# Queries and keys projected transposed and loaded whole, and readers moved away from producers, in a hybrid decoder step

## The chip, the core and the metric

The kernel runs on one core of one Trainium2 chip. The metric is the time of one execution on the device in microseconds (us). Engines are named as the profile names them: PE is TensorE (PEld its weight loads), DVE is VectorE, ACT is ScalarE, POOL is GpSimd, SP is SyncE, which here only issues DMAs. Each engine executes its own queue in order.

## What is computed

One layer of a decoder for two groups of rows that share weights: a prompt of 1024 rows, and a sample of 8 rows, each with 8192 cached positions.

```python
q, k, v, logf, u, z = mixer_inputs(rmsnorm(xp, g_mix[l]), w_in[l], b_f[l], g_sgu_v[l])
xp = xp + merge_heads(fox_prompt(q, k, v, logf), sgu_prompt(u, z, w_s[l], b_s[l]),
                      g_att_out[l], g_sgu_out[l], w_o[l])
mk, mv = memory_kv(mem_prompt, g_mem[l], w_ck[l], w_cv[l])
xp = xp + cross_attend(rmsnorm(xp, g_cross[l]), mk, mv, w_cq[l], w_co[l])
f, conv_p = conv_ffn(rmsnorm(xp, g_ffn[l]), ...)      # width-3 convolution, silu(gate) * val
xp = xp + f
...
att = fox_sample(q, k, v, logf, cache_k[l], cache_v[l], cache_logf[l], page_table)   # the sample's rows
```

`fox_attend` adds the difference of two cumulative sums of `logf` to each score, masks causally and takes a softmax over 8 heads of 64. `sgu_prompt` mixes the rows of each 128-row chunk with a causal 128x128 matrix per head and multiplies by u. Cross attention has 4 heads of 256 over 256 memory rows. The width is 1024, the MLP's is 2816. Outputs are the rows, and also the prompt's keys, values, gates, memory keys and values, and the last convolution rows.

## The kernel before

**Arithmetic.** Everything is float32. A large product is made of three fp32r products: `split` writes a high part (ScalarE, L212 or, with a gain, L215) and a low part, the rest (VectorE, L213 or L216), and `gemm3` (L242 to L244) adds high x high, high x low and low x high. `wload` (L230) loads a weight tile and splits it. Smaller products and all transposes run in float32.

**Stages of the prompt.** `p1` projects the normalised input in five column ranges: q, then gates and u, then k, v and z. The input comes transposed (`load_x`, L318); the row factors come from a second, row-wise load (`stats`, L328, squared in L207). q, k, v and the gating values go to DRAM (`evac`, L384 and L385). The decode's 8 sample rows ride along as narrow products (`sample_mm`, L254); `sample_sum` copies their parts out of PSUM (L266) and adds them up with one more product (L268).

Then the prompt goes in two halves of 512 rows. `attention` takes pairs of heads: `load` fetches q, k and v of a pair by rows, `setup` transposes q and k on TensorE (L649, L672), copies high parts (L655, L656, L676, L680, and POOL's L678) and subtracts low parts (L657, L681), so that one product over 128 rows and one over 68 rows (L696, L698; the last four rows carry the gate sums, fetched in L658 and L667) give a score; the exponentials are L706, the turning of the weights L724, the product with v L740. The first half's attention is mixed with the memory projection `pmem` and with `gating(0)`. Per half there follow `merge` and `out_proj` (with w_o), `cross`, which ends in another `out_proj` (w_co), and `ffn`. `residual` (L880, L207) adds each output tile to the rows and squares it; `norm_T` scales the rows (L920, before the MLP alone), transposes them (L929, L936) and splits them with the gain (L215, L216). In `cross`, `weigh` makes one head's weights (keys transposed in L977, scores L991, exponentials L997, scaling L1000) and `gather` turns them (L1008), copies them (L1009) and multiplies by the values (L1014).

**The sample.** `decode` walks 8 x 16 pieces of the cache: `kstep` gathers keys (L1175), multiplies by the query (L1183, on VectorE, and for some of the first 50 pieces on POOL) and sums (L1187); `vstep` gathers values (L1236) for column-tiled products (L1242). `sample_rest` then runs the eight rows through the remaining layers, to L1537 and the store in L1545.

**Order.** Both are generators. The prompt's yields a number after each piece of work; the loop at the end adds these up, and whenever the sum passes `PACE` of the stage (6 to 20; 4.0 once `sample_rest` has begun) it issues one step of the sample's. `mix` interleaves a second prompt generator in the same way. What is issued is a priority: a planner with a model of the engines fixes each engine's order. `hold`, set in `out_proj` where `i >= HI`, would stop the background; `HI` is 9 and i at most 3.

**Buffers.** 18 tiles of 128x1024 (`U`), 7 of 128x520 (`T2`), 4 raw weight tiles (`WRAW`), 4 and 2 PSUM banks that `BK` hands out in turn, one (`MS`) and one (`DV`) for the sample.

Of the kernel before, what the change touches and what calls it, by code (L numbers as in the profile page):

```python
# [22 lines left out]
NB = 8  # L23
# [35 lines left out]
KP = 2  # L59
PW = 1  # L60
LD = [(0, 1, 0), (0, 0, 0)]
ST = [(0, 1, 1), (0, 1, 1)]
# [7 lines left out]
HI = 9  # L70
HK = 0
# [3 lines left out]
SB = 2  # L75
# [8 lines left out]
def build(nc, tc, ctx, a, phases=None):  # L84
# [97 lines left out]
    q_d = dram.tile([T, AW], F32, tag="q_d", name="q_d")  # L182
    k_d, v_d = a["o_k"], a["o_v"]
# [3 lines left out]
    cq_d = dram.tile([NH, 4, T], F32, tag="cq_d", name="cq_d")  # L187
    ck_d = dram.tile([NH, 4, T], F32, tag="ck_d", name="ck_d")
# [74 lines left out]
    def sample_sum(ps, n, tmp=T2):  # L263

        t = tmp(n)
        nc.scalar.activation(t, ps[:, :n], AF.Copy)  # L266
        ps2 = BK()
        mmul(ps2[:8, :n], selS, t, start=True, stop=True)  # L268
        return ps2[:8, :n]
# [27 lines left out]
    def newest(e):  # L297

        return next(i for i in reversed(nc.cur_bb.bb.instructions) if i.engine == e)


    def p1(early):
        rstd = const.tile([P, 8], F32, tag="rstd", name="rstd")
        rstd8 = const.tile([P, 8], F32, tag="rstd8", name="rstd8")
        ssx = sm([P, 8], "ssx", 1)
# [6 lines left out]
        xh, xl = [[U([P, T], F32R) for _ in range(8)] for _ in range(2)]  # L312

        def load_x(kk, hf):
# [8 lines left out]
        def stats(hf):  # L323
            for q in range(2):
                xr = KV().rearrange("p (c d) -> p c d", d=D)
                t0 = hf * 4 + q * 2
                with tc.issue_after(x_in):
                    nc.sync.dma_start(xr, a["x"][t0 * P : (t0 + 2) * P, :].rearrange("(c p) d -> p c d", p=P))  # L328
                for i in range(2):
                    ssq_into(ssx[:, t0 + i : t0 + i + 1], xr[:, i, :])  # L330
            c = slice(hf * 4, hf * 4 + 4)
            r = rstd_of(ssx[:, c], D, 4, "r4")
            nc.vector.tensor_copy(rstd[:, c], r)
            nc.vector.tensor_scalar(rstd8[:, c], r, 0.125, None, op0=ALU.mult)
# [11 lines left out]
        def loaded(c0, n, parts, first=False):  # L346
# [3 lines left out]
            for kk in range(4):  # L350
                if first:
                    load_x(kk, 0)
# [3 lines left out]
                ws.append(w_)  # L356
                if first and kk == 1:
# [3 lines left out]

        ws, sps = loaded(O_Q, 512, [(0, 512)], first=True)
        for kk in range(4):
            load_x(kk, 1)
        x_in = newest(ENG.SP)
# [9 lines left out]
        stats(0)  # L375
        stats(1)
        sp = sample_sum(*sps[0])
        qs = T2()[:8]
        nc.vector.tensor_scalar(qs, sp, rs8, None, op0=ALU.mult)
        nc.sync.dma_start(qs_d, qs)  # L380

        def evac(ps, dst, sc, tt):
            t = T2()
            nc.scalar.activation(t, ps, AF.Copy, scale=sc[:, tt : tt + 1])  # L384
            nc.scalar.dma_start(dst[tt * P : (tt + 1) * P, :], t)  # L385

# [13 lines left out]
        pss = yield from by_rows(0, ws)  # L400
        for tt in range(8):
            ps = BK() if tt > 3 else pss[tt]
            if tt > 3:
                mm_chunk(tt, ws, ps, 0, 512)
                yield 5.2
            evac(ps, q_d, rstd8, tt)
# [32 lines left out]
        def gate_rows():  # L439
# [3 lines left out]
            for hf in range(2):  # L443
# [11 lines left out]
                for r_, src in ((0, ch), (1, cl)):  # L455
                    nc.sync.dma_start(cq_d[:, r_, s], src.bitcast(F32))
                    nc.sync.dma_start(cq_d[:, 2 + r_, s], one)
                    nc.sync.dma_start(ck_d[:, r_, s], one)
                    ng = T2()[:8]
                    nc.vector.tensor_scalar(ng, src.bitcast(F32), -1.0, None, op0=ALU.mult)  # L460
                    nc.sync.dma_start(ck_d[:, 2 + r_, s], ng)


        for c0, dst in ((O_K, k_d), (O_V, v_d)):
            ws, sps = loaded(c0, 512, [(0, 512)])
            for tt in range(8):
                ps = BK()
                mm_chunk(tt, ws, ps, 0, 512)
# [14 lines left out]
                evac(ps, dst, rstd, tt)  # L483
# [9 lines left out]
        for tt in range(8):  # L493
            if tt < 4:
                ps = BK()
                mm_chunk(tt, ws, ps, 0, 512)
                if tt == SD:
# [37 lines left out]
    def gating(hf):  # L535
# [6 lines left out]
        for pr_ in range(2):  # L542
            z = U([P, 2, 512])
            u = U([P, 2, 512])
# [3 lines left out]
            nc.sync.dma_start(u, sgu_d[rows, :].rearrange("(c p) d -> p c d", p=P))  # L548
            for i in range(2):
# [3 lines left out]
            yield 1  # L553
# [36 lines left out]
    def pmem():  # L590
        rm = const.tile([P, 2], F32, tag="rm", name="rm")
        ssm = sm([P, 2], "ssm", 1)
        for mt in range(2):
            t = U([P, D])
            nc.sync.dma_start(t, a["mem"][mt * P : (mt + 1) * P, :])
            ssq_into(ssm[:, mt : mt + 1], t)
        r = rstd_of(ssm, D, 2, "r2")
        nc.vector.tensor_copy(rm, r)
        mh, ml = [], []
        for q in range(2):  # L600
            h, l = U([P, 4, 256], F32R), U([P, 4, 256], F32R)
            raw = WRAW(1024).rearrange("p (k m) -> p k m", m=256)
            nc.sync.dma_start(raw, a["memT"][q * 512 : (q + 1) * 512, :].rearrange("(k p) m -> p k m", p=P))
            for k in range(4):
                kk = q * 4 + k
                split(raw[:, k, :], h[:, k, :], l[:, k, :], scale=gp[:, G_MEM + kk : G_MEM + kk + 1])
            mh.append(h)
            ml.append(l)
        yield 0.1
# [19 lines left out]
    def attention(hf, late=None, at=3):  # L629
# [3 lines left out]
        def load(hp):  # L633
            cs = slice(hp * P, (hp + 1) * P)
            qn = T2().rearrange("p (i c) -> p i c", c=P)
            nc.sync.dma_start(qn, q_d[hf * 512 : (hf + 1) * 512, cs].rearrange("(i p) c -> p i c", p=P))
            if hf == 0:
                kvn = U([P, 2 * nk, P])
# [1099 lines left out]
```

## Time and profile before

| | |
|---|---|
| median of 3 runs | 1971.17 us (1969.85 to 1985.79) |
| the profiled execution | 1971.44 us, span 1969.6 us |
| granted PE clock, mean | 0.965 |
| PE, DVE, ACT, POOL busy | 93%, 71%, 37%, 27% |
| DMA | 517 MB, mean 263 GB/s |

Stages in the span, by the first and last instructions of their lines: `p1` 0 to 277 us, the attention of the first half to about 385 and of the second to about 546, cross attention's products with the memory 661 to 723 and 1360 to 1420, the first MLP 816 to 1242, the second 1483 to 1945. The sample's decode ends at about 1515 and its rest at 1965. A busy share counts an instruction that runs at the half clock as busy, so 93% of PE holds slow work too; the column PEclk of a stretch tells how much.

### The profile page before, as it was taken

What the parts mean: (1) busy time and instruction counts of PE and PEld (TensorE: products, weight loads), DVE (VectorE), ACT (ScalarE), POOL (GpSimd) and SP (SyncE); (2) the same over time, 40 slices, a digit from 0 to 9 for tenths busy, and PEclk for the clock granted to TensorE, in tenths of its full rate; (3) what the DMA queues carried; (4) which work ended last, traced back from release to release, by engine and by line L of the source; (5) the groups of instructions that cost most, each with busy time, mean ns of one, the idle gap of its engine ahead of it and who ended that gap; (6) DMA issues with size and microseconds to landing.
All of it is one profiled execution on the core that took longest, in us unless ns stands there. A gap on an engine that the chain in (4) does not pass through costs nothing.

```text
span 1969.6 us, 23939 instructions
## 1 busy us (share of the span) xinstructions
PE 1828.8 (93%) x9159; PEld 1295.1 (66%) x9159; DVE 1395.3 (71%) x1651; ACT 730.1 (37%) x1344; POOL 538.0 (27%) x376
## 2 busy tenths in 40 slices
PE   8899989878899789699999999998999999999997
PEld 5777766556666547477777776666567677667773
DVE  4877466786767798898989999988335549653442
ACT  5332246566723232332432332433324333242331
POOL 1664342342245433323234243333110000000000
PEclk9999989989999989899999999999999999999998
DMA  8766777654487898788778798989664458665755
GB/s 327 257 242 211 290 303 244 244 166 142 161 342 275 325 335 324 249 324 299 291 268 336 271 356 339 374 314 363 232 217 151 150 188 273 233 220 211 271 192 193
DMA packets 160466, 517.05 MB, mean 263 GB/s; under 512 B 20168, under 2 KB 41928, under 8 KB 127584
## 3 DMA queue, kind: packets, MB, share of 16 engines
q0 software_dynamic: 38528, 270.88, 36.5%
q1 hardware_dynamic: 114912, 232.06, 33.8%
q10 hardware_dynamic: 6912, 12.59, 1.7%
q8 instruction: 72, 1.18, 0.2%
q14 instruction: 42, 0.34, 0.0%
HBM read 493.63 MB, written 21.84 MB: 262 GB/s over the span
## 4 chain that ended last, share of the span: by engine, by line
PE 71%; DVE 10%; DMA 9%; issue 5%; ACT 3%; POOL 1%; SPq 0%; ACTq 0%; DVEq 0%; POOLq 0%
PE ba L242 12%; PE ba L243 12%; PE ba L244 12%; PE bb L242 6%; PE bb L243 5%; PE bb L244 5%; PE dv L1242 5%; DVE s L1187 2%; DMA wr<-w_in 2%; DVE kv L1183 2%; DMA kv<-cache_k,kidx 2%; DVE wl L213 1%; PE dv L1485 1%; DMA u<-zg_d 1%; PE ba L1014 1%
## 5 line engine op out<-in xcount | busy, mean ns | idle before, releaser
L212 ACT ACTIVATE wh<-wr 128x1024 fp32r<-128x1024 f32 (+2 forms) x220 | 228.9, 1044 | 506.7 <-PE ba L243 176.5
L213 DVE TENSOR_TENSOR wl<-wr,wh 128x1024 fp32r<-128x1024 f32 (+2 forms) x220 | 268.5, 1231 | 176.7 <-PE ba L244 70.1
L1187 DVE TENSOR_REDUCE s<-kv 128x32 f32<-128x2048 f32 (+1 forms) x139 | 292.1, 2107 | 18.0 <-POOL kv L1183 17.4
L1175 POOL DMA_INDIRECT kv<-cache_k,kidx x128 | 174.3, 1362 | 449.1 <-PE dv L1242 208.4
L1236 POOL DMA_INDIRECT kv<-cache_v,kidx x128 | 182.5, 1426 | 354.3 <-PE dv L1242 224.7
L242 PE MATMUL ba<-wh,u 128*128 128x512 f32 (+1 forms) x674 | 262.4, 391 | 5.5 <-ACT u L212 2.8
L1183 DVE TENSOR_TENSOR kv<-kv,d 128x2048 f32<-128x2048 f32 (+1 forms) x109 | 248.2, 2282 | 24.8 <-DMA kv<-cache_k,kidx 23.7
L243 PE MATMUL ba<-wl,u 128*128 128x512 f32 (+1 forms) x674 | 258.7, 384 | 3.0 <-DVE wl L213 3.0
L244 PE MATMUL ba<-wh,u 128*128 128x512 f32 (+1 forms) x674 | 255.8, 383 | 0.2 <-DVE u L213 0.2
L242 PE MATMUL ba<-u,wh 128*128 128x512 f32 x568 | 227.4, 401 | 0.0
L244 PE MATMUL ba<-u,wl 128*128 128x512 f32 x568 | 225.9, 398 | 0.0
L243 PE MATMUL ba<-u,wh 128*128 128x512 f32 x568 | 225.1, 397 | 0.0
L242 PEld LDWEIGHTS ba<-wh,u 128*128 128x128 f32 x674 | 128.4, 190 | 54.0 <-issue 18.7
L243 PEld LDWEIGHTS ba<-wl,u 128*128 128x128 f32 x674 | 128.1, 190 | 33.9 <-issue 7.1
L244 PEld LDWEIGHTS ba<-wh,u 128*128 128x128 f32 x674 | 127.6, 189 | 28.9 <-issue 3.4
L1242 PE MATMUL dv<-kv,s 128*32 128x512 f32 x1024 | 135.2, 618 | 2.5 <-DMA kv<-cache_v,kidx 2.2
L1183 POOL TENSOR_TENSOR kv<-kv,d 128x2048 f32<-128x2048 f32 (+1 forms) x30 | 119.3, 3985 | 53.5 <-DMA kv<-cache_k,kidx 47.8
L242 PEld LDWEIGHTS ba<-u,wh 128*128 128x128 f32 x568 | 107.3, 189 | 40.4 <-issue 10.1
L244 PEld LDWEIGHTS ba<-u,wl 128*128 128x128 f32 x568 | 107.0, 188 | 34.5 <-issue 10.9
L243 PEld LDWEIGHTS ba<-u,wh 128*128 128x128 f32 x568 | 107.2, 189 | 33.3 <-issue 9.2
L242 PE MATMUL bb<-wh,u 128*128 128x512 f32 (+1 forms) x318 | 124.3, 391 | 1.6 <-ACT u L212 0.9
L243 PE MATMUL bb<-wl,u 128*128 128x512 f32 (+1 forms) x318 | 122.7, 386 | 1.0 <-DVE wl L213 1.0
(394 smaller groups left out, 2947.7 us busy)
## 6 DMA issues: line engine op xcount, KB each, us to landing
wr<-w_up SPq DMA_DIRECT2D x88, 512.0 KB
kv<-w_up SPq DMA_DIRECT2D x22, 1024.0 KB
wr<-w_down SPq DMA_DIRECT2D x40, 512.0 KB
kv<-w_down SPq DMA_DIRECT2D x11, 1024.0 KB
wr<-w_in SPq DMA_DIRECT2D x16, 512.0 KB
wr<-w_o SPq DMA_DIRECT2D x16, 512.0 KB
wr<-w_cq SPq DMA_DIRECT2D x16, 512.0 KB
wr<-w_co SPq DMA_DIRECT2D x16, 512.0 KB
```

The lines of the kernel that those rows point to most:

```text
L212: nc.scalar.activation(h, src, AF.Copy)
L213: nc.vector.tensor_tensor(l, src, h.bitcast(F32), op=ALU.subtract)
L242: mmul(out, sh, mh, start=(i == 0), stop=False)
L243: mmul(out, sh, ml, start=False, stop=False)
L244: mmul(out, sl, mh, start=False, stop=(i == n - 1))
L1014: mmul(ps, mv[:, mt, dd * P : (dd + 1) * P], pT[:, mt, :], start=(mt == 0), stop=(mt == 1))
L1175: nc.gpsimd.indirect_dma_start(kv, None, a["cache_k"], off(kidx[:, b, ch : ch + 1]))
L1183: eng.tensor_tensor(kvv[:, i : i + m, :], kvv[:, i : i + m, :], qb.unsqueeze(1).broadcast_to((P, m, 512)), op=ALU.mult)
L1187: nc.vector.tensor_reduce(s[:, ch * 4 + i : ch * 4 + i + m, :].rearrange("p k h -> p (k h)"), kvv[:, i : i + m, :].rearrange("p k (h d) -> ...
L1236: nc.gpsimd.indirect_dma_start(kv, None, a["cache_v"], off(kidx[:, b, ch : ch + 1]))
L1242: mmul(dv[32 * j : 32 * j + 32, :], s[:, ch * 4 : ch * 4 + 4, :].rearrange("p k h -> p (k h)"), kvv[:, j, :], start=(ch == 0), stop=(ch == ...
L1485: mmul(ps[32 * j : 32 * j + 32, q * 256 : (q + 1) * 256].rearrange("p (f c) -> p f c", f=2), xsT[:, k, :], rv[:, k], start=(k < 4), stop=( ...
```

## The change

**Projection.** q and k are projected with the weights stationary, so that they come out transposed (128 channels, which are two heads, by 512 rows). The row factors are made from the transposed input: ScalarE squares it, column-tiled products with ones add it up, and a product with a diagonal matrix spreads the factors over all partitions (`rrow`). `evac_T` scales, splits, and stores high and low parts in the two layouts that the score's two products read. The four gate rows are stored into the same tensors. Keys are also stored as an output, transposed, and the host turns that view.

**Attention.** `load` fetches the two operand tiles whole; `setup` with its transposes, copies and subtractions is gone.

**Readers and producers.** The sample's copy out of PSUM is issued one tile before the product that reads it. `out_proj` scales row tile i - 1 for the next norm (on ScalarE) before it adds tile i, and the last with high priority. `norm_T` transposes three row tiles, starts the next stage's first product on their 384 columns, and adds the last row tile's 128 afterwards; the weights of that product are requested ahead of it. `cross` is cut into `keys`, `weigh`, `turned` and `gather`, each issued a head ahead of its reader. `gating` and `pmem` load first, yield, and then compute; `gating(0)` uses raw weight tiles. The yields change with it.

```diff
-    q_d = dram.tile([T, AW], F32, tag="q_d", name="q_d")
-    k_d, v_d = a["o_k"], a["o_v"]
+    q1_d, k1_d = (dram.tile([NH, P, T], F32, tag=n_, name=n_) for n_ in ("q1_d", "k1_d"))
+    q2_d, k2_d = (dram.tile([NH, 68, T], F32, tag=n_, name=n_) for n_ in ("q2_d", "k2_d"))
...
+        def squares_in():
+            for k, x2 in x2s:
+                j = k % 4
+                mmul(sums[-1][32 * j : 32 * j + 32, :], ones[:, 0:32], x2, start=(k < 4), stop=(k >= 4), ...)
...
+        def evac_T(ps, hf, hp, scale, to1, to2, out=None):
+            c = slice(hf * 512, hf * 512 + 512)
+            t, h, l = T2(), T2(512, F32R), T2(512, F32R)
+            nc.vector.scalar_tensor_tensor(t, ps, scale, rrow[:, hf, :], op0=ALU.mult, op1=ALU.mult)
+            split(t, h, l)
+            x, y = (l, h) if out is None else (h, l)
+            heads = lambda dst, r0: dst[2 * hp : 2 * hp + 2, r0 : r0 + 64, c]
+            nc.scalar.dma_start(heads(to1, 0), h.bitcast(F32))
+            nc.scalar.dma_start(heads(to1, 64), x.bitcast(F32))
+            nc.scalar.dma_start(heads(to2, 0), y.bitcast(F32))
+            if out is not None:
+                nc.sync.dma_start(out[hp * P : (hp + 1) * P, c], t)
...
+            if tt == SD - 1:
+                sps = [sample_copy(*sp) for sp in sps]
             if tt == SD:
                 sp = sample_sum(*sps[0])
...
+            q1, q2 = U([P, 2, 512], F32R), U([P, 2, 512], F32R)
+            heads = slice(2 * hp, 2 * hp + 2)
+            nc.sync.dma_start(q1.bitcast(F32), q1_d[heads, :, qc].rearrange("h p t -> p h t"))
             if hf == 0:
...
+                k1, k2 = U([P, 2, 512], F32R), U([P, 2, 512], F32R)
...
+                ka, kb = ([U([P, nk * P], F32R) for j in range(2)] for _ in range(2))
...
+            vn = (T2() if hf == 0 else U([P, nk * P])).rearrange("p (i c) -> p i c", c=P)
...
-        def setup(hp, qn, kn, vn):
...
+        def prepare(i):
+            r = rows_rstd(sq, i, i + 1)
+            y = U([P, D])
+            for c in (slice(0, 512), slice(512, D)) if i == 3 else (slice(0, D),):
+                nc.scalar.activation(y[:, c], xt[i][:, c], AF.Copy, scale=r)
+            ys.append(y)
...
+    def norm_T(ys, g0, first):
...
+            split(tr[:, 0:384], hs[-1][:, 0:384], ls[-1][:, 0:384], scale=gp[:, g0 + kk : g0 + kk + 1])
+            if kk % 2:
+                yield 0.8
+        first(hs, ls, slice(0, 384))
+        yield 4
...
+        first(hs, ls, slice(384, 512))
         return hs, ls
...
+        keys(0)
+        keys(1)
+        yield 1
+        weigh(0)
+        yield 3
+        weigh(1)
+        yield 3
+        for h in range(MH):
+            if h + 2 < MH:
+                keys(h + 2)
+            turned(h)
+            yield 1
+            if h:
+                gather(h - 1)
+                yield 4
+            if h + 2 < MH:
+                weigh(h + 2)
+                yield 3
+        gather(MH - 1)
...
     def gating(hf):
...
-            z = U([P, 2, 512])
-            u = U([P, 2, 512])
+            z, u = (U([P, 2, 512]) if hf else WRAW(1024).rearrange("p (c d) -> p c d", d=512) for _ in range(2))
...
+            yield 6
...
-            yield 1
+            yield 3
```

More of the change, by code (lines that the diff above doesn't have):

```diff
@@ L74 @@
 LT = 3
-SB = 2
 KS = 2
@@ L943, in norm_T, with products @@
+            yield 0.6
+        first(hs, ls, slice(384, 512))
         return hs, ls
     def cross(xt, sq):
-        hs, ls = yield from norm_T(xt, None, G_CROSS)
+        ws = [wload(wpair(a["w_cq"], kk, 0, 512), 1024) for kk in range(4)]
+        q2, ps0 = [], MM()
+        def products(out, ws, dt_, hs, ls, c):
+            cb = slice(dt_ * P, (dt_ + 1) * P)
+            gemm3(
+                out,
+                [(ws[k // 2][0][:, k % 2, cb], ws[k // 2][1][:, k % 2, cb], hs[k][:, c], ls[k][:, c]) for k in range(8)],
+            )
@@ L1114, in build @@
     last = {}
-    hold = [False]
     bgs, acc, phase = [], [0.0], ["p1", None]
@@ L1640, in build @@
         acc[0] += t
-        while bgs and not hold[0] and acc[0] >= PACE[phase[1] or phase[0]]:
+        while bgs and acc[0] >= PACE[phase[1] or phase[0]]:
             acc[0] -= PACE[phase[1] or phase[0]]
```

397 lines of the change are left out of this document (211 added, 186 removed).

## The prediction

> **What bounds the kernel now.** I read four views: the page's busy shares and slices, the stretches by stage, the waits of TensorE, and the timeline at two stage boundaries.
>
> ```profile
> PE 1828.8 (93%) x9159; PEld 1295.1 (66%) x9159; DVE 1395.3 (71%) x1651; ACT 730.1 (37%) x1344; POOL 538.0 (27%) x376
> ...
> PEclk9999989989999989899999999999999999999998
> ```
>
> TensorE is the bound: it is idle for 1969.6 - 1828.8 = 141 us. The busy figure also hides slow work: where the granted clock of a stretch is c, (1 - c) of the stretch is work not done. The stages show where:
>
> ```profile
> core 0: us, PE busy (x) PEld busy (x) DVE busy (x) ACT busy (x) POOL busy (x), PEclk, DMA share, GB/s
> ...
> 277.00:385.00 108.00, 89.58 (x470) 65.66 (x468) 68.44 (x121) 64.77 (x145) 34.41 (x31) 0.91 0.77 271
> 385.00:546.00 161.00, 135.57 (x886) 93.86 (x885) 120.89 (x244) 106.59 (x281) 57.18 (x57) 0.93 0.50 167
> ...
> 661.00:723.00 62.00, 42.57 (x185) 24.67 (x184) 53.26 (x64) 21.85 (x52) 19.39 (x15) 0.85 0.90 334
> ...
> 790.00:816.00 26.00, 10.35 (x54) 6.44 (x54) 21.52 (x30) 7.34 (x15) 11.75 (x10) 0.67 0.75 265
> 816.00:1242.00 426.00, 425.05 (x1994) 307.93 (x1992) 396.84 (x358) 145.91 (x229) 135.00 (x91) 1.00 0.83 310
> ```
>
> These are the first and second half's self-attention, the first half's cross attention, its step into the MLP, and the MLP. The MLP is full (425 of 426 us) and the change doesn't reach inside it. In the other four, 357 us long, TensorE is idle for 79 us and loses 10 + 11 + 9 + 9 = 39 us to the half clock. No other engine is full there except VectorE in cross attention (53 of 62 us) and at the MLP step (21.5 of 26). So latency between engines is the limit there, and the waits name it:
>
> ```profile
> PE ba L929 <- DVE u L920: 11.0, 1, 11.0
> PE ba L1014 <- ACT u L1009: 7.8, 3, 6.5
> PE ba L696 <- ACT wr L706: 7.4, 6, 2.7
> PE ba L696 <- ACT u L680: 7.0, 1, 7.0
> ...
> PE bb L268 <- ACT t L266: 5.1, 1, 5.1
> PE ba L696 <- DVE u L681: 4.1, 3, 2.4
> PE ba L268 <- ACT t L266: 3.7, 1, 3.7
> ```
>
> The 11.0 us is the MLP step: the transposes (L929) stand right behind the scaling of the rows (L920), and VectorE is late with all of it, because weight splits and a decode multiply are queued ahead of the residual sum (L880) that everything needs:
>
> ```profile
> 788.62 1.21 DVE L213 TENSOR_TENSOR wl<-wr,wh 128x1024 fp32r<-128x1024 f32 x1
> 789.75 2.27 DVE L1183 TENSOR_TENSOR kv<-kv,d 128x2048 f32<-128x2048 f32 x1
> ...
> 793.22 0.67 DVE L880 TENSOR_TENSOR u<-ba,u 128x512 f32<-128x512 f32 x1
> ```
>
> **The sum, part by part**, against this execution's own 1971.4 us (span 1969.6; the median of the three runs is 0.3 us below).
>
> (a) *Start: row sums from the transposed input.* Added on TensorE: 16 column-tiled products (eight of that kind, L1242, take 1.07 us together in the timeline, so 2.1), two all-ones products (0.43 us apart, L1014's spacing, about 1) and eight one-column ones (up to 0.1 each). About +4 us, bounds 2 to 8. ScalarE squares 16 times 512 columns (0.68 each, 11 us) in place of 8 times 1024 (8.4); it is busy 23 of the first 37 us, so this hides, and would cost 2.6 us if not. The 4.2 MB of rows no longer read (14 us at 299 GB/s) hid already: TensorE waits for nothing over 0.3 us between 7 and 73 us.
>
> (b) *Sums of the sample's parts.* The copy out of PSUM now stands a tile ahead of the product that reads it. Idle 5.1 + 3.7 = 8.8, and the clock of the two stretches around them (0.96 of 83 us, 0.97 of 50) costs 4.8 more. The cover is one tile of products (5.4 us). Bounds 0 and -14; I take -11.
>
> (c) *Evacuating q and k.* Per tile one copy (L384, 0.69 on ScalarE) becomes a scaled pass on VectorE (0.74 by L472, also from PSUM), a ScalarE copy (0.63) and a VectorE subtraction (0.69). In the k stage (120 to 170 us) VectorE is busy 40.1 of 50 and gets 8 x 1.43 = 11.4 more: full. Six PSUM banks at 5.5 us per tile take up some 25 us of lateness, and the v stage has room (58.9 of 107). But VectorE slows beside GpSimd: an 8x512 product (L476) takes 4.17 us beside a GpSimd multiply and 0.68 elsewhere. Three such multiplies lie in the k stage, so up to three subtractions can take 4 us more. The ScalarE queue issues 48 stores for 16 (L385, 0.34 us: 11 us more, ScalarE busy 45 of 133), the SyncE queue 8 more; k's stores grow from 0.26 to 1.05 MB per tile, some 140 GB/s on the 222 moved, about the most that a slice of the page reached (374). A store of a low part waits on ScalarE's queue for VectorE's subtraction, and ScalarE's next copies wait behind it. What is late then are decode's gathers, not the projection. Bounds 0 and +12; I take +4.
>
> The Trainium skill (SBUF — State Buffer, "Who interferes with whom") says more exactly that a VectorE instruction with two SBUF inputs contends with GpSimd reads, and one with a single SBUF input does not. By it only the subtraction suffers, not the pass from PSUM: +12 at most; without it the pass could too, +24.
>
> (d) *Attention.* Gone from TensorE: 80 transposes of 128 columns, 0.11 us apart: -8.7. Gone from ScalarE are 64 copies (L655, L656, L676, L680: 37.7 us of 171), from VectorE 40 subtractions (27.4 of 189), from GpSimd 16 casts and 32 DMA issues of 0.6 us that stood ahead of decode's gathers. The first pair's wait of 7.0 and some of the 10 us that the clock costs the first half: queries and keys are now loaded while the last projection runs; -8 (-3 to -12). Waits for setup later (L681 4.1, L657 3.6): -8 (-3 to -8). The rest, waits for the exponentials (about 16 us) and the rest of the 21 us lost to the clock, shrinks as its engines lose a fifth of their work: -13 (0 to -24). What it costs: a pair now loads 1.9 MB (first half) or 2.9 MB (second) for 0.75 and 1.3, and each set holds 4 or 7 of the 18 big buffers from load to last use; v takes one of the 7 small ones in the first half, for a whole pair. +4 (0 to +20). Together -34.
>
> (e) *Four norm steps.* The first product is split into 384 and 128 columns: 512 columns stand 0.231 us apart, 260 stand 0.120, so 384 some 0.175; 128 lies between a quarter of 0.231 and 0.120, and I take the transposes' 0.11: 24 x (0.175 + 0.11 - 0.231) = 1.3 us each, +5 in all (0 to 6). Gain: rows 0 to 2 are scaled a tile early on ScalarE, and their transposes (24 x 0.11) and first product (4.2) lie over the last row's chain, which is residual, square, power and scaling: about 5 us when nothing is queued ahead. In the MLP step TensorE idles 15.7 of 26; the decode multiply before the residual stays, so -11. The second half's step idles 5.4 and runs at clock 0.66 for 15 us: -5. Before cross attention 3.2 and 2.3 are idle: -3. Together -14, with gains bounded by 8 and 27.
>
> The Trainium skill (TensorE: Matmul & The Clock Gate, "Back-to-back issue gap") gives about 81 ns for 128 columns and 131 ns for 512. This trace's 512 take 231 ns, so the row decides; with 81 the split would cost 0.6 us each, 2.4 in all.
>
> (f) *Cross attention.* Each head's transposes and products move a head away from what they read. Idle 19.4 of 62, clock 0.85. VectorE's 53 us are a floor, less 6 us of gating that moves to the end: at most 62 - 47 = 15 can go. -9; for the second half (7.3 idle of 64) -5. Together -14 (-4 to -22).
>
> (g) *Background pace.* Decode steps are issued by the sum of the yields. Added up by hand, gating's and the norms' longer yields bring 3 more steps before the first MLP, each 4.4 us of VectorE (L1183 2.28, L1187 2.11): 0 to +13 where VectorE is near full, I take +4. The same sum lets the decode end some 22 yields sooner against the program's end.
>
> (h) *Tail.* Today the prompt's last store is issued at 1949.1 and the sample's chain runs on alone:
>
> ```profile
> 1951.47 1.93 PE L1524 MATMUL dv<-kv,d 128*32 128x512 f32 x4 [3.16 <-DMA kv<-w_down]
> ...
> 1958.68 1.88 PE L1537 MATMUL ba<-d,cp 128*8 128x512 f32 x4 [0.70 <-ACT d L1535]
> ```
>
> Its stores are issued at 1964. Ending 22 yields sooner it lies inside the MLP; the 15 us go, its products (3 us warm) come back: -9 (0 to -15).
>
> The rest costs nothing: `hold` was never set (HI is 9, i at most 3).
>
> Sum: +4 - 11 + 4 - 34 - 14 - 14 + 4 - 9 = -70, so 1901 us.
>
> **Rivals.** *VectorE takes the place of the waits (1943 us).* In-order VectorE with decode ahead of residuals is what the MLP step shows (789.75 to 793.22), and it was busy 61 of 67 us from 723 to 790. If the boundary and cross gains (19 + 14) go and (g) costs its full 13, 1901 + 33 + 9 = 1943. Against it: ScalarE, busy 7 of 26 us there, takes the scaling.
>
> *More than forecast (1857 us).* If attention, cross attention, tail and sums reach their good ends (-19, -8, -6 and -3 more) and (c) and (g) cost nothing (-8), 1901 - 44. For it speaks that TensorE is idle for 44 of attention's 269 us while no engine there is over 85% busy.
>
> *Loading whole defeats the prefetch: slower (2021 us).* In the second half's attention two sets take 14 of 18 big buffers, the output 2, the turned weights 2 to 4. If fewer than a full set is free when a load is issued, until the pair before has done its values, the load starts when it is needed: 2.9 MB at the 167 GB/s left of 334 is 17.5 us, 1.9 MB 11 us; three pair changes in each half, 86 us, with the attention gain gone too: 1901 + 34 + 86. It decides from the point where a set is not free by the time half a pair (20 us) has run. By my count it is just free: the first head's two k tiles are released before the last turned weights need theirs.
>
> **How the numbers follow.** About 1% (20 us) is what a measurement of this kernel can tell from no change. Forecast 0.60 (own range 1865 to 1935, all faster); VectorE in the way 0.22, from 1930 to 1965: 0.13 faster, 0.09 same; more than forecast 0.10; prefetch defeated 0.08, slower. Faster 0.60 + 0.13 + 0.10 = 0.83. The range 1855 to 1960 leaves out the slow rival and the outer ends of the other two. All bounds at their bad ends give about 2004, at their good ends 1843; neither comes all at once.
>
> **What would show it.** Right: no wait of the sample product for its copy; no setup group in attention and a clock there of 0.95 or more; the MLP step under 16 us; TensorE idle for 60 to 80 us; the prompt's final store among the last. Wrong: TensorE waiting in attention for DMA of q1 or k1; tile buffers held until late; the scaled pass of k late by tens of us with idle time behind it; VectorE waits at the MLP step as long as now.

## The result, and the profile after

The changed kernel takes 2206.3 us (median of 4 runs, 2204.5 to 2208.6) against 1974.4 for the kernel before in the same comparison: a ratio of 1.117, with a 95% interval of 1.113 to 1.120. The prediction was 1901 us, faster. The profiled execution's span is 2203.1 us, 233.5 more than before. Its page, in the lines shown of before:

```profile
PE 1868.6 (85%) x9227; PEld 1311.0 (60%) x9227; DVE 1395.8 (63%) x1671; ACT 708.8 (32%) x1324; POOL 491.9 (22%) x332
...
PEclk9667966897969998997999999999999999999999
```

TensorE is idle for 2203.1 - 1868.6 = 334 us instead of 141, and the low clock (6 and 7 tenths) now lies in the first quarter. The stages of after, and below them the projections of before:

```profile
core 0: us, PE busy (x) PEld busy (x) DVE busy (x) ACT busy (x) POOL busy (x), PEclk, DMA share, GB/s
0.00:45.00 45.00, 37.94 (x144) 21.71 (x146) 21.03 (x52) 26.89 (x42) 9.05 (x13) 1.00 0.81 282
45.00:487.00 442.00, 261.68 (x1249) 193.59 (x1246) 174.37 (x150) 71.16 (x109) 105.56 (x50) 0.78 0.44 153
487.00:767.00 280.00, 213.59 (x1264) 146.36 (x1262) 159.37 (x310) 136.77 (x358) 65.54 (x43) 0.87 0.69 232
892.00:954.00 62.00, 49.99 (x219) 27.93 (x221) 57.30 (x67) 22.68 (x56) 23.96 (x18) 0.92 0.92 342
1010.00:1058.00 48.00, 25.96 (x129) 17.23 (x128) 42.59 (x55) 14.10 (x29) 16.86 (x14) 0.72 0.83 321
1058.00:1479.00 421.00, 418.66 (x1942) 299.76 (x1941) 387.99 (x354) 140.59 (x222) 132.27 (x89) 1.00 0.81 304
```

```profile
45.00:277.00 232.00, 222.13 (x1200) 173.23 (x1199) 157.10 (x112) 70.31 (x102) 118.65 (x55) 0.98 0.70 252
```

The projections (45 to 487, before 45 to 277) take 210 us longer, and every column there is low: VectorE 174 and ScalarE 71 of 442 us, the DMA engines 44% busy. Nothing is full, so something in order must be waiting. The other stages change by 22 us or less each: attention +15, output projection and cross attention -5, the stretch to the MLP +22, all after it -8. TensorE's waits (waiter, what it waited for; us, times, longest) name ScalarE and the row tiles:

```profile
PE ba L267 <- ACT t L261: 42.9, 2, 23.3
PE bb L238 <- ACT wh L208: 25.5, 2, 14.4
PE bb L238 <- DVE t L425: 24.0, 2, 22.9
PE bb L667 <- DVE u L649: 22.5, 1, 22.5
PE ba L238 <- DVE t L425: 19.9, 1, 19.9
PE ba L667 <- DVE u L659: 13.7, 1, 13.7
```

L425 is `evac_T`'s scaled pass, L208 `split`'s copy, L261 the sample's copy, L649 and L659 gating. What ScalarE does when it is "not busy" is in its timeline in the k stage (start, duration; ACTq is its sequencer issuing a DMA):

```profile
245.81 0.64 ACT L208 ACTIVATE t<-t 128x512 fp32r<-128x512 f32 x1 [1.07 <-DVE t L425]
246.47 0.50 ACTq L430 DMA_DIRECT2D k_d<-t  x1
247.01 0.51 ACTq L431 DMA_DIRECT2D k_d<-t  x1
247.62 4.05 ACTq L432 DMA_DIRECT2D k_d<-t  x1
263.64 0.64 ACT L208 ACTIVATE t<-t 128x512 fp32r<-128x512 f32 x1 [17.19 <-DMA k_d<-t]
...
271.19 5.16 ACTq L430 DMA_DIRECT2D k_d<-t  x1
276.38 8.02 ACTq L431 DMA_DIRECT2D k_d<-t  x1
284.50 3.18 ACTq L432 DMA_DIRECT2D k_d<-t  x1
287.78 0.63 ACT L208 ACTIVATE t<-t 8x512 fp32r<-8x512 f32 x1 [16.62 <-DMA k_d<-t]
```

One store of 256 KB holds ScalarE's sequencer for up to 8 us in these lines, where the prediction had 0.34 (L385 of before); the longest of the run took 15.8 us (durations in ns: min, median, max):

```profile
L431 ACTq DMA_DIRECT2D k_d<-t x8: 513/4474/15775, 247.0 to 384.8; - x8
```

Over all 48 stores the issues add up to 225 us, close to the loss. The next copy waits on top of that for a row buffer that an unfinished store still reads: of the 17.19 us ahead of the copy at 263.64, which a DMA to k_d ended, about 5 are the three issues and 12 are this wait. Why a store is slow is in the DMA queues' lines (packets, MB, share of 16 engines) for ScalarE's queue, before and after:

```profile
q10 hardware_dynamic: 6912, 12.59, 1.7%
```

```profile
q10 hardware_dynamic: 10848, 20.97, 2.5%
```

Before, all 48 stores on this queue are of 128 rows of 2 KB: 6912 / 48 = 144 packets, 128 of data and 16 of 4 bytes. After, 32 are of that kind, and the new 48 have (10848 - 32 x 144) / 48 = 130: 128 and 2. Counted packet by packet, two data packets of this queue are in flight at a time during 217 us, and sixteen during 5. A packet of 2 KB takes 84 ns, so 64 on each of two engines take 5.4 us, and 48 such stores 258 us. This is how `dst[2 * hp : 2 * hp + 2, r0 : r0 + 64, c]` is moved: its outermost dimension is 2. The Trainium skill states it (DMA: Bandwidth & Descriptors, "Why a DMA increments its semaphore by 16 and not by 1" and "Rules for kernel authors"): a DMA uses the largest number of engines, at most 16, that divides the slowest dimension of both sides. The packet counts agree: 16 extra packets for a store of 128 rows, 2 for these. The prediction overlooked it.

### The profile page after: what moved, and what is told of

It is laid out like the page before. It is cut to its first block, busy times and chain, and to the rows that moved or that the text cites. A ratio compares the mean times of both kernels' runs of the same rounds, so it can differ in the third digit from the quotient of the medians.

```text
span 2203.1 us, 24093 instructions
## 1 busy us (share of the span) xinstructions
PE 1868.6 (85%) x9227; PEld 1311.0 (60%) x9227; DVE 1395.8 (63%) x1671; ACT 708.8 (32%) x1324; POOL 491.9 (22%) x332
## 3 DMA queue, kind: packets, MB, share of 16 engines
q10 hardware_dynamic: 10848, 20.97, 2.5%
## 4 chain that ended last, share of the span: by engine, by line
PE 60%; DVE 7%; DMA 5%; issue 1%; ACT 1%; POOL 1%; SPq 0%; DVEq 0%; POOLq 0%; ACTq 0%
PE ba L238 10%; PE ba L240 10%; PE ba L239 10%; PE bb L238 5%; PE bb L239 5%; PE bb L240 5%; PE dv L1355 4%; DMA u<-wsT 2%; DVE s L1300 2%; DVE kv L1296 2%; DMA t<-o_mk 1%; PE dv L1598 1%; PE bb L808 1%; DVE wl L209 1%; PE ms L824 1%
## 5 line engine op out<-in xcount | busy, mean ns | idle before, releaser
L209 DVE TENSOR_TENSOR wl<-wr,wh 128x1024 fp32r<-128x1024 f32 (+2 forms) x220 | 279.1, 1276 | 185.7 <-PE ba L240 50.5
L208 ACT ACTIVATE wh<-wr 128x1024 fp32r<-128x1024 f32 (+2 forms) x220 | 229.0, 1044 | 519.2 <-PE ba L239 147.2
L1288 POOL DMA_INDIRECT kv<-cache_k,kidx x128 | 159.7, 1248 | 658.1 <-DVE s L1300 388.8
L1300 DVE TENSOR_REDUCE s<-kv 128x32 f32<-128x2048 f32 (+1 forms) x138 | 292.3, 2122 | 4.3 <-POOL kv L1296 3.8
L238 PE MATMUL ba<-wh,u 128*128 128x512 f32 (+1 forms) x616 | 242.3, 395 | 43.3 <-DVE t L425 19.9
L238 PE MATMUL ba<-u,wh 128*128 128x512 f32 (+2 forms) x608 | 241.8, 404 | 12.9 <-DVE snT L584 10.2
L1296 DVE TENSOR_TENSOR kv<-kv,d 128x2048 f32<-128x2048 f32 (+1 forms) x108 | 236.1, 2190 | 17.6 <-DMA kv<-cache_k,kidx 16.8
L239 PE MATMUL ba<-u,wh 128*128 128x512 f32 (+1 forms) x608 | 242.4, 399 | 0.0
L240 PE MATMUL ba<-u,wl 128*128 128x512 f32 (+1 forms) x608 | 241.3, 398 | 0.0
L239 PE MATMUL ba<-wl,u 128*128 128x512 f32 (+1 forms) x616 | 240.0, 391 | 0.3 <-DVE wl L209 0.3
L240 PE MATMUL ba<-wh,u 128*128 128x512 f32 (+1 forms) x616 | 237.1, 389 | 0.0
L238 PEld LDWEIGHTS ba<-wh,u 128*128 128x128 f32 x616 | 120.4, 196 | 88.3 <-issue 20.2
L238 PE MATMUL bb<-u,wh 128*128 128x512 f32 (+2 forms) x352 | 137.7, 392 | 24.0 <-DVE t L425 24.0
L238 PEld LDWEIGHTS ba<-u,wh 128*128 128x128 f32 x608 | 114.9, 191 | 53.3 <-issue 12.1
L239 PEld LDWEIGHTS ba<-wl,u 128*128 128x128 f32 x616 | 120.5, 196 | 32.5 <-issue 10.5
L239 PE MATMUL bb<-u,wh 128*128 128x512 f32 (+2 forms) x352 | 138.4, 393 | 0.1
L240 PEld LDWEIGHTS ba<-wh,u 128*128 128x128 f32 x616 | 119.8, 195 | 31.3 <-issue 9.2
L1296 POOL TENSOR_TENSOR kv<-kv,d 128x2048 f32<-128x2048 f32 (+1 forms) x30 | 120.1, 4011 | 79.4 <-DMA kv<-cache_k,kidx 73.0
L240 PE MATMUL bb<-u,wl 128*128 128x512 f32 (+2 forms) x352 | 137.5, 391 | 0.0
```

What stands on the lines that cost most here:

```text
L208: nc.scalar.activation(h, src, AF.Copy)
L209: nc.vector.tensor_tensor(l, src, h.bitcast(F32), op=ALU.subtract)
L238: mmul(out, sh, mh, start=(i == 0), stop=False)
L239: mmul(out, sh, ml, start=False, stop=False)
L240: mmul(out, sl, mh, start=False, stop=(i == n - 1))
L1288: nc.gpsimd.indirect_dma_start(kv, None, a["cache_k"], off(kidx[:, b, ch : ch + 1]))
```

## The experiments

**The stores alone, on the changed kernel (e1, e4) and on the kernel before (e2, e3, e9).** e1 issues each store as two, one for each head:

```diff
-            heads = lambda dst, r0: dst[2 * hp : 2 * hp + 2, r0 : r0 + 64, c]
-            nc.scalar.dma_start(heads(to1, 0), h.bitcast(F32))
...
+            for dst, r0, s_ in ((to1, 0, h), (to1, 64, x), (to2, 0, y)):
+                for j in range(2):
+                    nc.scalar.dma_start(dst[2 * hp + j, r0 : r0 + 64, c], s_[64 * j : 64 * j + 64].bitcast(F32))
```

> Each of the 48 stores of evac_T is issued as two, one for each head, with 64 rows as the outermost dimension instead of 2; bytes, buffers and the queue stay. Theory (two DMA engines): on ScalarE's queue the changed kernel moves 130 packets per such store, 128 of data and 2 more, where the kernel before moves 144, 128 and 16; and two packets are in flight at a time for 217 us. So a store of 64 packets on each of two engines at 84 ns takes 5.4 us, 48 take 258 us, and ScalarE's queue, TensorE's clock and the row buffers wait for that. With the split the issue falls from some 5 us to 0.3 to 0.5 us, and of the about 210 us by which attention starts later most comes back: 1960 to 2040 us. Rival (bytes, or the number of issues): twice as many issues and the same bytes, 2200 us or more. Rival (the passes on VectorE beside GpSimd, or seven row buffers for three tiles per block): nothing changes, 2190 to 2220.

Measured: 2024.0 us, ratio to before 1.025 (1.018 to 1.031). e4 keeps high and low parts in scratch of their own, so that a tile needs two stores of 128 rows, and lets the loads put the operands together:

```diff
-            nc.scalar.dma_start(heads(to1, 0), h.bitcast(F32))
...
+            nc.scalar.dma_start(to_h[hp * P : (hp + 1) * P, c], h.bitcast(F32))
+            nc.scalar.dma_start(to_l[hp * P : (hp + 1) * P, c], l.bitcast(F32))
```

> The changed kernel with the high and low parts in scratch of 512 x 1024 each, so that a tile is stored with two DMAs of 128 rows instead of three of 2 x 64, and the loads put the operands together (high part of k read twice, gate rows apart). Theory (two DMA engines): 1950 to 2030 us, 0 to 10 under the split version, for 32 issues instead of 96. Rival (passes on VectorE, or buffers): 2180 or more, since both stay as they are.

Measured: 2002.8 us, 1.012 (1.005 to 1.018). So e1, which changes the stores alone, gives back 182 of the 232 us, and e4 203; e4 also makes two stores of three and loads the operands in more pieces, and what the 21 us between the two are was not tested. The issues of after, e1 and e4, one line each (min, median and max in ns):

```profile
L432 ACTq DMA_DIRECT2D q_d<-t x8: 495/5732/7595, 57.1 to 181.9; - x8
```

```profile
L431 ACTq DMA_DIRECT2D q_d<-t x48: 452/607/1895, 61.0 to 110.4; - x48
```

```profile
L428 ACTq DMA_DIRECT2D qh_d<-t x8: 326/326/345, 61.7 to 99.4; - x8
```

The converse, in the kernel before, where neither the passes on VectorE nor the three tiles per block exist. Each tile of q and k is stored three more times into scratch that nothing reads, in three forms of the same 12.6 MB:

```diff
+                for i in range(3):
+                    nc.scalar.dma_start(more[n, i, :, 0:64, :], t)   # e2: 2 x 64 rows
+                    nc.scalar.dma_start(more[n, i, :, 0:32, :], t)   # e9: 4 x 32 rows
+                    nc.scalar.dma_start(more[n, i], t)               # e3: 128 rows
```

> The kernel before, with three more stores of each evacuated tile of q and k into scratch, in the changed kernel's pattern (outermost dimension 2); nothing reads them. Theory: 48 x 5.4 = 260 us more on ScalarE's queue, against some 50 us a projection of slack: 2100 to 2210 us, issue times of about 5 us, clock at half for over 250 us. Rival (the passes on VectorE, or the buffers for three tiles): the passes are not here, 1975 to 2000. Rival (bytes): as e3.

> As e2, with the scratch split in four instead of two (outermost dimension 4, pieces of 32 rows). Theory (as many engines as the outermost dimension says, 84 ns a packet of 2 KB): 32 packets each on four engines, 2.7 us a store instead of 5.4; 132 packets per store on ScalarE's queue instead of 130; 24 of 48 stores' time lies on top of a projection's 5.5 us per tile only in part, so far less than half of e2's 195 us: 1985 to 2060 us. Rival (any store in pieces is slow): as e2, 2150 or more.

> The kernel before, with the same three more stores of each tile into scratch that lies as the tile does (128 rows as the outermost dimension); nothing reads them. Theory: 48 more issues of 0.34 us, 16 us of a ScalarE that is busy a third of these stages: 1972 to 1995 us. Rival (bytes: 12.6 MB more): as e2, 2050 or more.

Measured: 2168.2 us with two pieces (1.097, 1.090 to 1.104), 2054.8 with four (1.040, 1.035 to 1.046), 1975.9 with 128 rows (1.0005, 0.998 to 1.003). Their issues, in that order:

```profile
L390 ACTq DMA_DIRECT2D more<-t x48: 500/4992/12169, 41.7 to 384.6; - x48
```

```profile
L390 ACTq DMA_DIRECT2D more<-t x48: 511/2335/11353, 42.1 to 278.9; - x48
```

```profile
L390 ACTq DMA_DIRECT2D more<-t x48: 326/466/1040, 42.2 to 200.6; - x48
```

From four pieces to two the issue doubles, as it would if the store ran on half as many engines; the bytes of 48 more stores of 128 rows cost nothing that can be measured. The rivals (bytes, the passes beside GpSimd, the row buffers by themselves) are out: the passes and the buffers are the same in e1 and e4, and the bytes in e2 and e3. Two things stay untested: how the loss divides between the held queue and the buffers that come free late, and what the same stores would cost if SyncE issued them.

**Gating (e8).** With the stores repaired, 100 us of the forecast are still missing. e4's longest waits are gating's product:

```profile
PE bb L664 <- DVE u L646: 19.4, 1, 19.4
PE ba L664 <- DVE u L656: 10.9, 1, 10.9
PE ba L1076 <- DMA t<-o_mk: 10.4, 1, 10.4
```

e8 is e4 with `gating` as it was:

```diff
-            z, u = (U([P, 2, 512]) if hf else WRAW(1024).rearrange("p (c d) -> p c d", d=512) for _ in range(2))
+            z = U([P, 2, 512])
+            u = U([P, 2, 512])
...
-            yield 6
...
-            yield 3
+            yield 1
```

> e4 with gating as in the kernel before. Theory (the new gating): the 19.4 us wait of its product in attention and the 10.9 us at the MLP step go, with some 18 us lost to the half clock around them: 1950 to 1975 us. Rival (big buffers: the triangular weights wait for one of 18 that attention's whole operands hold, whatever the yields): the wait in attention stays, 1980 to 2000 us.

Measured: 1964.9 us, 0.995 (0.992 to 0.997). Some 35 us are there (38 by the medians, 33 by the ratios), but only half of the reason holds: the second call leaves the MLP step, while the first still waits 16.3 us in attention, now for its inputs (L656 scales z) instead of its weights:

```profile
PE bb L664 <- DVE u L656: 16.3, 1, 16.3
```

**The two halves alone (e5, e6, e7).** e5 is e8 without the second half: `pmem`, `out_proj`, `norm_T`, `cross` and `ffn` are those of before. e6 and e7 are the kernel before with the second half and the sums of the sample's parts, with gating new (e6) or as before (e7).

> Only the first half of the change, with whole stores as in e4: q and k projected transposed, row sums from the transposed input, operands loaded whole, sums of the sample parts a tile apart; gating, the memory's setup, the four norm steps and cross attention are as before. The prediction's sum for this part is 4 - 11 + 4 - 34 = -37, some 1936 us. Theory after e4 (its TensorE idles 60 of the 274 us from the last projection to the end of attention, where the kernel before idles 44 of 265, and its start takes 15 us more): the part gives nothing or costs a little without the gating's wait, 1975 to 2005 us.

> Only the second half: projections and attention as before, with the sums of the sample parts, gating, the memory's setup, the four norm steps and cross attention as in the changed kernel. The prediction's sum for this part is -11 - 14 - 14 + 4 - 9 = -44, some 1929 us. Theory (gating's second call now falls into the step to the MLP, 10.9 us of idle TensorE in e4, and the decode runs ahead of it): 1935 to 1960 us, with an idle stretch of about 10 us ahead of gating's product at the MLP step. Rival (the step costs as much as it gives): 1965 to 1980.

> As e6, with gating as in the kernel before (its tiles in the big buffers, yields of 1 instead of 6 and 3). Theory: gating stays in cross attention, the step to the MLP is free of it: 10 to 20 us less than e6, 1920 to 1945 us. Rival (gating isn't what holds the step): as e6.

Measured: e5 1961.1 us, 0.992 (0.989 to 0.995), the lowest median of all; e6 1981.7, 1.004 (1.002 to 1.006); e7 1978.5, 1.003 (1.000 to 1.005). e8's interval overlaps that of e5, so that which of the two is faster is not shown. So the first half gains 12 us (16 by the ratio) of the 37 forecast, and the second loses 5 (e7) to 8 (e6) instead of gaining 44; the expectations for e6 and e7 were too good. The step from e6 to e7 is the same edit of `gating` as from e4 to e8, and here it gives 3 us instead of some 35: what the new gating costs depends on the whole loads beside it, and by itself it costs nothing that can be measured.

TensorE's idle time ahead of its instructions is 132 us in before, 130 in e5, 127 in e7 and 127 in e8. The waits that were aimed at did shrink, and others grew, also in code that is the same (in e5 gating and the decode's products):

| TensorE idle ahead of (us) | before | e5 | e7 | e8 |
|---|---|---|---|---|
| sums of the sample's parts | 8.9 | 2.3 | 0.0 | 1.4 |
| scores | 23.2 | 3.0 | 15.5 | 3.7 |
| cross attention, its four parts | 22.0 | 10.7 | 9.1 | 13.5 |
| norm steps' transposes | 21.8 | 14.6 | 20.9 | 17.8 |
| gating | 3.1 | 15.7 | 11.6 | 16.3 |
| turned weights (`turn`) | 11.5 | 17.6 | 7.8 | 18.5 |
| the decode's products with cached values | 2.5 | 17.4 | 10.8 | 5.7 |
| fp32r products | 11.2 | 16.8 | 19.5 | 17.7 |

The equal totals prove little. These are single executions that took 1966 to 1973 us, with TensorE busy for 1826 to 1835 of them; where the time differs, the idle time does too (152 us in e4 at 2003, 122 in e14 at 1960). More telling is which chain ends last. In e5 the prompt's last product and the sample's last one are:

```profile
1933.28 0.40 PE L242 MATMUL ba<-wh,u 128*128 128x512 f32 x1
...
1955.25 1.02 PE L1619 MATMUL ba<-d,cp 128*8 128x512 f32 x2
```

The prompt ends at 1934 us in e5, against 1945 in before, 11 us sooner. But the sample's chain runs on alone, with 12.8 us of a DMA of `w_down` in it, and the span of this execution is only 5 us shorter. In e7 the prompt ends at 1958, 13 us later than in before, and the sample's last product at 1962 instead of 1961: the second half made the prompt slower, and the shorter tail hid it.

**The first pair (e10).** In e5 TensorE idles 13.6 us from 306, ahead of the first turned weights. No engine is busy there but the DMA's (columns as in the stages above):

```profile
300.00:320.00 20.00, 4.92 (x23) 3.74 (x22) 4.78 (x6) 6.13 (x14) 2.96 (x3) 0.72 1.02 347
```

Two pairs' whole operands, the memory's weights and decode's gathers are moved at once. e10 requests the second pair later:

```diff
-LD = [(0, 1, 0), (0, 0, 0)]
+LD = [(1, 0, 1), (0, 0, 0)]
```

> e5, with the second pair's operands of the first half requested five eighths into the first pair instead of three eighths. Theory (burst of transfers): between 280 and 320 us of e5 the DMA engines are over 100% busy at 300 to 408 GB/s with two pairs' operands, the memory's weights and decode's gathers, z's stores wait behind them (no packet on ScalarE's queue from 290 to 310), and TensorE idles 13.6 us from 306; with the second pair later the stretch shrinks below 6 us: 1940 to 1958 us. Rival (the row buffers, one of which holds v for a whole pair): the stretch stays, 1955 to 1968 us. A later load may also come too late for the second pair: then a wait of TensorE on its operands, and no gain.

Measured: 1963.6 us, 0.995 (0.992 to 0.998). The stretch shrinks to 4.5 us as the theory says, but the time doesn't follow: the burst fits as the cause of that wait, and the wait is not what sets the end. In the profile of e10 the prompt's last product ends at 1931 us, the sample's at 1953.

**The decode at the MLP step (e11, e13, e12, e14, e15).** The prediction's rival had VectorE in the way there. e11 holds the decode's steps back while the last rows are finished:

```diff
                 residual(xt, sq, i, n, ps)
+                paused[0] = ys is not None and n == 1 and i > 0
...
-        while bgs and not hold[0] and acc[0] >= PACE[phase[1] or phase[0]]:
+        if bgs and not paused[0] and acc[0] >= PACE[phase[1] or phase[0]]:
```

> e7, with the decode's steps held back from the second row tile of the second half of the output projection until the norm step is over, and caught up with at most one a yield after it. Theory (the rival VectorE of the prediction: residual, sum and power of the last row stand behind decode multiplies of 2.3 us each on VectorE): TensorE's idle time in the step to the MLP (13.6 of 38 us in e7) falls below 7 us and its half clock of 20 us below 10, the second half's step a little: 1955 to 1972 us. Rival (the chain through ScalarE and the weight splits is what takes the time): 1972 to 1985, the idle time stays.

Measured: 1992.6 us, 1.008 (1.006 to 1.011). The `if` also slowed the sample's later stages, and its last product ended 39 us behind the prompt's. e13 limits the decode alone to one step a yield:

> e11 with the limit of one background step a yield for the decode alone, so that the sample's later stages run at e7's pace. Theory (VectorE's decode steps ahead of the last row are what takes the gain of the norm steps): the step to the MLP stays at some 22 us with under 7 of idle time, the sample again ends within 15 us of the prompt: 1952 to 1970 us. Rival (decode's VectorE and TensorE work takes the same time wherever it is put): the 16 us come back in the MLP or at the end, 1972 to 1985.

Measured: 1979.1 us, 1.001 (0.998 to 1.004). The step and the MLP behind it, first in e7, then in e13:

```profile
793.00:832.00 39.00, 25.36 (x114) 17.66 (x113) 30.93 (x39) 14.42 (x29) 12.62 (x11) 0.74 0.75 273
832.00:1257.00 425.00, 420.18 (x1972) 299.85 (x1970) 390.94 (x356) 144.09 (x227) 154.06 (x92) 1.00 0.81 305
```

```profile
790.00:814.00 24.00, 18.74 (x104) 16.12 (x103) 12.49 (x27) 12.39 (x27) 2.94 (x3) 0.86 0.35 135
814.00:1244.00 430.00, 424.81 (x1986) 299.61 (x1984) 406.55 (x365) 147.79 (x231) 166.10 (x100) 1.00 0.85 319
```

VectorE's 31 busy us in the step become 12, and the step shrinks from 39 to 24 us, with idle time of 5 instead of 14. So VectorE was in the way. But the gain does not last: the MLP takes 5 us more, its end is 13 us sooner than in e7, the prompt's last product 3.5 us sooner (1954.1 against 1957.6) and the sample's last one 1.2 us later (1963.2 against 1962.0). The two medians differ by less than 1 us. The theory of e13 holds for the place and its rival for the total; that it is the decode's work that comes back in the stages behind the MLP is not shown. The same edit on the others: e12 and e14 are e8 with e10's edit and the one of e11 or e13; e15 is e10 with before's `hold` set from the second row tile on and at most one step a yield.

> The whole change with the three repairs: stores of 128 rows (e4), gating as before (e8), the second pair's operands later (e10) and the decode held at the steps (e11). If the repairs add to e8's 1965: -5 to -12 for the loads and -5 to -15 for the steps, 1940 to 1955 us. If either theory fails, 1955 to 1970.

> e12 with the same edit as e13. Theory: e12's 1982 less what its slowed end costs (some 20 us), and under e8 by the step's gain: 1940 to 1962 us. Rival (as in e13): as e8, 1962 to 1975.

> e10 (first half of the change alone, repaired) with the decode held back from the second row tile of the second half of each output projection until the first transposes of the norm step, and caught up one step a yield. Theory: 4 to 10 us less idle time at the step to the MLP (7.5 and 5.0 us of TensorE's idle time lie at 780 and 794 in e10), 1948 to 1960 us. Rival (the same work later): as e10, 1958 to 1970.

Measured: e12 1982.1 us, 1.006 (1.003 to 1.008); e14 1965.5, 0.996 (0.993 to 0.999); e15 1965.4, 0.993 (0.990 to 0.997). None is faster than e5, and the repairs don't add up.

## Why the prediction was wrong

**The step that failed is (c), evacuating q and k.** It took the 48 stores at 0.34 us an issue, the row of a store of 128 rows, and the bytes at the rate of all engines, and put +4 us (0 to 12) on all of (c). That the new stores begin with a dimension of 2 stood in the diff; the issue cost 4.9 us in the median, and the term was 182 us (after against e1) to 203 us (after against e4). "What is late then are decode's gathers, not the projection" was the wrong way round: the projection's own TensorE waited for buffers. The sign that the prediction named, "the scaled pass of k late by tens of us with idle time behind it", is what the profile shows. The rest of (c) held. In e4 the scaled passes (L425) and the subtractions (L209), min, median and max in ns:

```profile
L425 DVE SCALAR_TENSOR_TENSOR t<-bb,u x8: 671/678/684, 60.3 to 190.9; 128x512 f32<-128x512 f32 x8
L425 DVE SCALAR_TENSOR_TENSOR t<-ba,u x8: 671/681/684, 62.3 to 205.4; 128x512 f32<-128x512 f32 x8
```

```profile
L209 DVE TENSOR_TENSOR t<-t,t x18: 660/692/4937, 61.7 to 208.8; 128x512 fp32r<-128x512 f32 x16, 8x512 fp32r<-8x512 f32 x2
```

Two subtractions took 3.8 and 4.9 us, both beside a GpSimd multiply, where (c) had "up to three" at 4 us more. Not every one beside such a multiply is late: of nine in e1, e4 and e8, four took 3.8 to 4.9 us and five 0.68 to 0.69. None of the passes from PSUM was: of 8 that lay beside a GpSimd multiply in after, e1, e4, e5 and e8, the longest took 0.69 us. That is the rule of the Trainium skill that the prediction weighed (SBUF — State Buffer, "Who interferes with whom"), by which only the subtraction can suffer, and the trace agrees with it. In after no subtraction happened to lie beside one.

**(b)** held in kind: TensorE's idle time for the sums went from 8.9 to 3 us or less wherever the stores were repaired. In the changed kernel it is the longest wait (42.9 us), since the copy (L261) stands behind the stores on ScalarE.

**(a)** was too low: in e5 the start and the projections take 20 us more than before (297 for 277), where (a) and (c) forecast 8. Idle time is 6 us of it, and most of the rest is the row sums, a term that was mis-sized:

```profile
L331 PE MATMUL ms<-t,ones 128*32 128x512 f32 x32 | 13.1, 658 | 7.2 <-DMA wr<-w_in 7.2
...
22.00 1.03 PE L331 MATMUL ms<-t,ones 128*32 128x512 f32 x4
```

The 16 column-tiled products stand in the profile as 32 records, two for each, and the "eight of that kind" of L1242 in 1.07 us were four products. Moreover L1242 issues four column tiles together, and `squares_in` two: four records, or two products, take 1.03 us. The 32 are busy for 13.1 us where (a) had 2.1, the two all-ones products (L367) for 3.2 where it had 1, and the one-column ones (L352) for 2.0 where it had up to 0.8. Against before, the records of this column-tiled form take up some 10 us more of TensorE's time.

**(d)** In e5 attention takes 248 us for 265: -17 instead of -34. The waits for setup are gone as forecast (scores 23.2 to 3.0), but "the first pair's wait" is not: two whole sets saturate the DMA engines there, a cost that stood inside the +4 (0 to 20). Gating's product waits 12.6 us longer too.

**(e)** At the full clock the split cost 24 x (0.20 + 0.112 - 0.231), some 2 us each instead of 1.3; 384 columns stand 0.20 us apart on average (0.17 to 0.31). The gain of 11 at the MLP step did not come: in after the step runs from 1010 to 1058, 48 us for 26. Gating's second call is one part of it: its product waits 13.7 us there (L667). The other part is VectorE's order, with the sum of squares of the last row (L959) and its scaling (L196) among decode's multiplies and reductions (L1296, L1300):

```profile
1017.30 2.29 DVE L1296 TENSOR_TENSOR kv<-kv,d 128x2048 f32<-128x2048 f32 x1
1019.50 0.14 DVE L1344 COPY lT<-ms 8x1 f32<-8x1 f32 x1
1019.57 0.14 DVE L959 TENSOR_TENSOR rq<-sqx 128x1 f32<-128x1 f32 x1
1019.63 2.28 DVE L1300 TENSOR_REDUCE s<-kv 128x32 f32<-128x2048 f32 x1
1021.83 0.14 DVE L196 TENSOR_SCALAR rn3r<-rq 128x1 f32<-128x1 f32 x1
1021.89 2.28 DVE L1296 TENSOR_TENSOR kv<-kv,d 128x2048 f32<-128x2048 f32 x1
```

This was the rival of 1943 us, "VectorE takes the place of the waits", and by e13, which has gating as before, its mechanism at this place is right. To let ScalarE scale the rows leaves these two short VectorE instructions in the chain, each behind a decode step of 2.3 us.

**(f)** -11 in after (892 to 951 for 661 to 731), inside its bounds, though `keys` now waits 10.5 us for a DMA once. **(g)** and **(h)**: the tail behind the prompt's last product fell from 25 us to 9 in after and 14 in e7, where the prompt itself ended later; in e5 it grew to 31. That the decode steps that moved forward took the time elsewhere is not shown. In e5, e7 and e8 the sample's stores are still the last. In after it is the prompt's, as forecast (L1225, behind the sample's L1658), in SyncE's timeline:

```profile
2193.78 0.96 SPq L1658 DMA_DIRECT2D o_ys<-dec  x2
2197.11 2.66 SPq L1225 DMA_DIRECT2D o_y<-u  x3
```

**Gating**, which the sum had at "VectorE, less 6 us that moves to the end", cost some 35 us beside the whole loads (e4 against e8) and about 3, inside the noise, without them (e6 against e7): that term was missing.

**The slow rival** (loading whole defeats the prefetch, 2021 us) named the wrong place: TensorE never waits long for q1 or k1. What whole loads delay, as far as e5's profile shows, is what stands behind them: VectorE idles 9.8 us for a load of z (`zg_d`) ahead of gating's scaling (L658).

So the sum failed by a term of 182 to 203 us from one DMA pattern. Of the 102 us that e4 still lacks, gating is some 35, and the start, (a), some 10 by e5's rows, an estimate. The rest was forecast as gain, wait by wait; in the repaired versions other waits took the place of those that went, and the sample's chain, not the prompt's, ended last in e5, e7 and e8. Why the new waits come to about as much as the old ones is left open.

## What to carry to other kernels

Cost a DMA by its access pattern before its bytes: here outermost dimensions of 2, 4 and 128 rows came with 2, 4 and 16 extra packets a store and issues of 4.99, 2.34 and 0.47 us, and the queue's packet count shows which one a kernel has. A slow store that is issued from an engine that computes holds up that engine's queue as well. Count the records of a product before taking a price from them. And price a removed wait by what would wait next, and by the chain that ends last: in the profile of e5, 11 us gained by the prompt were 5 at the end, where the sample's chain ran on.

## What was not expected of the hardware

An issue of a slow store holds the engine that makes it: on ScalarE one took up to 15.8 us (after) and 12.2 us (e2), against 0.33 for the same bytes over 16 engines (e4, median). In the timeline above two issues of 0.5 us come ahead of one of 4.05, which fits a queue that takes some stores and then holds the issuer until it has caught up; no run tests that. A store of 64 rows, also over 16 engines, was issued in 0.61 us, one of 128 rows in 0.33 (e1, e4): half the bytes took twice the issue. e1's 96 stores took 63 us of ScalarE's queue, e4's 32 took 11; whether this is the 21 us between the two was not tested.
